# Two fused transformer blocks on one core: where the modulation products run

## The chip, the core and the metric

The kernel runs on one core of one Trainium2 chip, as one program of 31743 instructions. The metric is the device time of one execution in microseconds (us). Engines are called by the names of the profile: PE (TensorE, matmul), PEld (its weight loads), DVE (VectorE), ACT (ScalarE), POOL (GpSimd) and SP (SyncE, which here only issues transfers).

## The reference, cut to what matters

Two transformer blocks follow each other on 512 tokens of width 1024, in float32. The first block begins with a modulation: six vectors of 1024 numbers, made from a conditioning vector `c` and a 1024 x 6144 matrix.

```python
mod = jax.nn.silu(c) @ ada_w[l] + ada_b[l]
sh_m, sc_m, g_m, sh_f, sc_f, g_f = jnp.split(mod[:, None, :], 6, axis=-1)
h = rmsnorm(x, norm_g[l, 0]) * (1.0 + sc_m) + sh_m
p = h @ w_in[l]
...
x = x + g_m * rmsnorm(y, norm_g[l, 1])
h = rmsnorm(x, norm_g[l, 2]) * (1.0 + sc_f) + sh_f
f = conv_ffn(h, ffn_up[l], ffn_conv_w[l], ffn_conv_b[l], ffn_down[l])
x = x + g_f * rmsnorm(f, norm_g[l, 3])
```

`sh_m` and `sc_m` are wanted before the first projection; the other four are wanted only after the mixers. The mixers are a chunked RWKV recurrence (4 heads), a forgetting attention ("fox", 6 heads) and a sparse attention ("nsa", 6 heads, with compressed keys and values). The second block (a feed-forward, a token mixer, a feed-forward) uses no modulation, and nothing in it changes.

## The kernel before

**Layout.** Activations lie feature by token, in eight tiles of 128 features x 512 tokens. Each float32 operand of a projection is split into a high and a low part: `uh` and `ul` for activations, `whi` (ACT, L273) and `wlo` (DVE, L274) for weights. `dense` (L434) does three matmuls for each block of 128 x 128 weights. The weights come from one long stream of 128 x 1024 pieces, loaded by SP in program order into three buffers called `raw` (L268); `whi` and `wlo` have three buffers each.

**Front** (L543 to L601). Bias lines for the nsa bias come first (`lines`, L468): a one-hot table is loaded in four pieces of up to 512 columns, cast on POOL (L481), multiplied on PE, and written to DRAM (`d1`). The sum of squares of x gives the norm (`R`). Then for each of the eight feature blocks k, `products(k)` (L566) loads two 128 x 1024 pieces of the modulation matrix (`aw`, seven buffers) and multiplies them on PE, as 16 matmuls of 128 x 256 with a strip of 32 columns each (`silz`), into the bank `mps`. `modulate(k)` (L577) copies the strips (`am`), adds them up with four matmuls against a column of ones, and makes `mod`, `gf`, `uf` (DVE) and then `uh` (ACT) and `ul` (DVE). After that come 21 matmuls of block k into seven accumulators `kps` (called k in the profile). `products(k + 1)` is written ahead of the first of these, `modulate(k + 1)` ahead of the fourth.

**Preparation** (`prep`, L727, two head pairs), with projection matmuls as filler (`fill`, L949).

**Core** (loop over `core(t)`, L800, the chunk recurrence of the two head pairs). At each turn the loop takes a step of the recurrence, some filler projections (tile psm), and three steps of a side list: `decays`, `compress` (L990: tiles kk, kr, psa, ch, kct), then `fox` (L1102: tiles pss, p, pt). Every second turn `some_ada` (L616) emits one of the 16 late modulation units through `ada` (L503): two pieces of 128 x 1024 go into the same three `raw` buffers that the weight stream uses; the four terms of the first piece are made on DVE (one multiply, three multiply-adds), the first term of the second piece on ACT, and its other three on POOL (a multiply and an add each, L518 and L519), then one add joins both (L520). Two matmuls against ones (tile psr) and two adds give `mod`. In `compress`, POOL adds a position term to the gathered keys (`kr`, L1002). In `fox`, POOL scales the softmax rows (`p`, L1120). `load_cb` (L961) issues eight small transfers on POOL's queue.

What sets the order: the program is scheduled ahead of time by a list scheduler with priorities. Each engine then runs its own list strictly in order, so an instruction that waits holds all behind it on that engine; the same holds for transfers on SP's and POOL's queues.

Of the kernel before, what the change touches and what calls it, by code (L numbers as in the profile page):

```python
# [279 lines left out]
def two_blocks(ctx, tc, ins, out):  # L280
    nc = tc.nc
    S, V, G, PE = nc.scalar, nc.vector, nc.gpsimd, nc.tensor
    def mm(o, l, r, start=True, stop=True):
        PE.matmul(o, l, r, start=start, stop=stop)  # L284

    def act(o, i, f, **kw):
        S.activation(o, i, f, **kw)  # L287
# [10 lines left out]
    def stt(o, a, s, b, op0, op1):  # L298
        V.scalar_tensor_tensor(o, a, s, b, op0=op0, op1=op1)  # L299
# [156 lines left out]
    def lines_in(name, pool, rb, n, h, tiles=None):  # L456

        l = pool.tile([33, h], F32, name="rb" + name)
        V.memset(l[32:33, :], 1.0)
        (G if tiles else nc.sync).dma_start(l[:32, :], ins[rb])  # L460
        cols = []
        for j in range(0, n if tiles else 0, 512):
            m = min(512, n - j)
            cols.append(tiles()[:33, :m])
            G.dma_start(cols[-1], ins["lines" + name][:, j:j + m])
        return l, cols

    def lines(name, pool, o_tile, pst, n, h, dst, l, cols):  # L468

        hi, lo = [pool.tile([33, h], F32R, name="rb" + name + c) for c in "hl"]  # L470
        act(hi, l, AF.Copy)
        tt(lo, l, hi.bitcast(F32), SUB)
        for j in range(0, n, 512):
            m = min(512, n - j)
            if cols:
                o = cols.pop(0)
# [26 lines left out]
    def ada(dst, sec, k, raw, ap, bufs):  # L503

        am = [ap.tile([P, 256], F32, name=f"am{q}", bufs=bufs) for q in range(2)]
        for q in range(2):
            aw = raw()
            nc.sync.dma_start(aw.rearrange("p a b -> p (a b)"), ins["ada"][sec, k][:, q * 1024:(q + 1) * 1024])
            for r in range(4):
                s = sil[:, 4 * q + r:4 * q + r + 1]  # L510
                if q == 0 and r:
                    stt(am[0], aw[:, r], s, am[0], MUL, ADD)
                elif q == 0:
                    ts(am[0], aw[:, 0], s, None, MUL)
                elif r == 0:
                    act(am[1], aw[:, 0], AF.Copy, scale=s)
                else:
                    G.tensor_scalar(aw[:, r], aw[:, r], s, 1.0, op0=MUL, op1=MUL)  # L518
                    G.tensor_tensor(am[1], am[1], aw[:, r], op=ADD)  # L519
        G.tensor_tensor(am[1], am[0], am[1], op=ADD)  # L520
        for s in range(2):
            c = slice(s * P, (s + 1) * P)
            mm(dst[s], am[1][:, c], ones[:, 0:1])
# [16 lines left out]
    vcn = keep.tile([31, 2, 64], F32, name="vcn")  # L540
    cmask = keep.tile([P, 256], BF16, name="cmask")
    us = []
    AWB = 7  # L543
    with tc.tile_pool(name="lin", bufs=1) as lin, tc.tile_pool(name="p0", bufs=1, space=PSUM) as p0:
        x0 = part
        l1 = lines_in("1", keep, "rel_bias", E1_N, 6, lambda: lin.tile([P, T], F32, name="l1", bufs=4))
        for i in range(4):
            nc.sync.dma_start(x0[:, 2 * i:2 * i + 2], ins["x"][:, 2 * i:2 * i + 2])
        q0 = SqSum()
        for k in range(8):  # L550
            q0.add(x0[:, k])
        ps = row_sums(p0.tile([P, T], F32, name="nst", tag="x0"), [q0.acc])
        msx = const.tile([P, NB], F32, name="msx")
        V.tensor_copy(msx, ps[:, :NB])
        R = rms_bcast(p0, "x0", rsq(msx))
        kps = [p0.tile([P, T], F32, name=f"k{m}") for m in range(7)]
        spare = iter(kps[3:])
        lines("1", keep, lambda dt: lin.tile([P, T], dt, name="lo", bufs=3), lambda: next(spare), E1_N, 6, d1, *l1)
# [5 lines left out]
        mps, ws = [None] * 8, [None] * 8  # L564

        def products(k):  # L566


            mps[k] = p0.tile([P, T], F32, name="mps", tag="x0")
            for q in range(2):  # L570
                aw = lin.tile([P, 4, 256], F32, name="aw", bufs=AWB)
                nc.sync.dma_start(aw.rearrange("p a b -> p (a b)"), ins["ada"][0, k][:, q * 1024:(q + 1) * 1024])
                for r in range(4):
                    mm(mps[k][32 * r:32 * r + 32, :256], silz[:, 4 * q + r], aw[:, r], q == 0, q == 1)
            ws[k] = W.next("rwkv")

        def modulate(k):  # L577
            ps = mps[k]
            cp = lin.tile([P, 256], F32, name="am", bufs=2)
            V.tensor_copy(cp, ps[:, :256])  # L580
            for s in range(2):
                mm(ps[:, 256 + s:257 + s], cp[:, s * P:(s + 1) * P], ones[:, 0:1])
            tt(mod[:, k:16:8], ps[:, 256:258], vc("ada_b", 0, 16)[:, k::8], ADD)
            stt(gm[:, k:k + 1], mod[:, 8 + k:9 + k], 1.0, vc("norm_g", k), ADD, MUL)
            t = tmp("uf")
            stt(t, x0[:, k], gm[:, k:k + 1], R, MUL, MUL)
            us.append(cut_by(t, None, mod[:, k:k + 1], two(k)))

        products(0)
        modulate(0)  # L590
        for k in range(8):
            hi, lo = ws[k]
            for m in range(7):
                if k < 7 and m == 0:
                    products(k + 1)
                if k < 7 and m == 3:
                    modulate(k + 1)
                dense(kps[m], hi, lo, m * P, us[k:k + 1], k == 0, k == 7)
        for m in range(7):
            act(pr[m], kps[m], AF.Identity, scale=omu[:, m:m + 1])  # L600
            stt(pr[m][:, 1:], kps[m][:, :T - 1], vc("mu", m), pr[m][:, 1:], MUL, ADD)  # L601
# [11 lines left out]

    todo = [(sec, k) for sec in (1, 2) for k in range(8)]

    def some_ada(n=1):  # L616
        for _ in range(min(n, len(todo))):
            ps = bank(f"r{len(todo) % 2}", 2)
            sec, k = todo.pop(0)
            ada([ps[:, 0:1], ps[:, 1:2]], sec, k, lambda: wpool.tile([P, 4, 256], F32, name="raw", bufs=W.raw_bufs), st, 2)  # L620
            for s in range(2):
                j = (2 * sec + s) * 8 + k
                tt(mod[:, j:j + 1], ps[:, s:s + 1], vc("ada_b", j), ADD)

    def proj_t(label, evac):
        hi, lo = W.next(label)
# [333 lines left out]

    def load_cb():  # L961
        for p1 in range(8):
            G.dma_start(cb[p1 * 16:(p1 + 1) * 16],
                              bass.AP(tensor=d1[:].tensor, offset=d1[:].offset + LN + 7 - p1,
                                      ap=[[LC, 16], [E1_N, 6], [1, 55]]))

# [23 lines left out]
    def compress(spare):  # L990

        for j, nm in enumerate(("k", "v")):
            pe = vc("pe_" + nm, 0, 16)
            krs = [spare("kr") for _ in range(2)]
            for g in range(2):
                kk = spare("kk2")
                nc.sync.dma_start(kk[0:64], kcv[j][H2[g]])
                nc.sync.dma_start(kk[64:128, :T - 1], kcv[j][H2[g], 1:])
                kv = kk.rearrange("p (c j l) -> p c j l", j=8, l=2)[:, :, :, 0].rearrange("p c j -> p j c")
                for a in range(2):  # L1000
                    kr = krs[a][:, :496].rearrange("p (j g c) -> p j g c", g=2, c=31)
                    G.tensor_tensor(kr[:, :, g], kv[:, :, a:a + 31],  # L1002
                                    pe[:, 8 * a:8 * a + 8, None].to_broadcast([P, 8, 31]), op=ADD)
            ps = bank("a", 1)
            for q in range(4):
                w1 = spare("w1")
# [95 lines left out]
    def fox(j, spare):  # L1102
# [7 lines left out]
        for i in range(NB):  # L1110
# [3 lines left out]
            for s in range(2):  # L1114
                ps = pS()
                mm(ps[:, :n], fq[j][H2[s], qs], fk[j][H2[s], :n], True, False)
                mm(ps[:, qs], cmask[:, :P], cmask[:, P:], False, True)
                p = tmp("p")
                r = soften([(ps[:, :n], fb[s][:, :n])], p)
                G.tensor_scalar(p[:, :n], p[:, :n], r, 1.0, op0=MUL, op1=MUL)  # L1120
                yield
                pts.append(flip(p, n, spare("pt")))
            yield
# [309 lines left out]
    def raw(name, k, s, hl):  # L1433

        return cut_by(x[k][:, s], vc(name, k), None, hl, s)
# [597 lines left out]
```

## Time and profile before

| | |
|---|---|
| time, median of 3 runs | 2218.21 us (2211.95, 2218.21, 2218.94) |
| the profiled execution's own time | 2212.43 us |
| its span, first to last instruction | 2210.6 us |
| PE busy | 2140.8 us (97%) |
| DVE busy | 1141.6 us (52%) |
| ACT busy | 787.0 us (36%) |
| POOL busy | 440.7 us (20%) |

A busy share is a mean over the whole span. The stages differ, so the profile is read by stretch: the front ends at 80.68 us, when the first matmul into psm begins; the core begins at about 133 us and ends at about 376 us; from 600 us to the end PE is busy almost without a gap. "Idle before" with a name behind an arrow is the time that an engine stood still, and what it was waiting for. PEclk is the granted clock of TensorE, 1.00 for 2.4 GHz and 0.50 for 1.2 GHz.

### The profile page before, as it was taken

The numbers are of one execution on the slowest core, as the hardware profiler recorded it, in microseconds if no ns is written. First come the engines' busy times: TensorE is split into PE (matmuls) and PEld (weight loads), VectorE is DVE, ScalarE is ACT, GpSimd is POOL, SyncE is SP. The second block draws the span as 40 slices with busy tenths as digits, with TensorE's granted clock in tenths as the row PEclk, the third lists the DMA queues.
The fourth block names the chain that finished last, engine by engine and source line by source line (L and its number), as shares of the span: only waits on it lengthen the run. The fifth ranks groups of instructions, "written<-read, shape, count | busy, mean of one in ns | idle before, by whom it ended". The sixth has DMA issues, their size and how long they took to land.

```text
span 2210.6 us, 31743 instructions
## 1 busy us (share of the span) xinstructions
PE 2140.8 (97%) x12572; PEld 1761.8 (80%) x12572; DVE 1141.6 (52%) x2191; ACT 787.0 (36%) x1326; POOL 440.7 (20%) x444
## 2 busy tenths in 40 slices
PE   7988999998999999899999999999999999999999
PEld 4777776766788888888888889998877888888887
DVE  4563544657653465654344439967645455433442
ACT  3332233553543343332222335445443233222221
POOL 2043343235000000221011023343221022100110
PEclk9987998998999999999999999999999999999999
DMA  8244233301452222132222343243162223322222
GB/s 318 77 141 148 97 135 97 113 1 32 151 181 97 96 95 96 58 109 101 96 95 95 119 142 113 92 139 96 67 186 68 101 85 101 103 96 96 96 95 86
DMA packets 84319, 238.32 MB, mean 108 GB/s; under 512 B 13270, under 2 KB 20887, under 8 KB 84042
## 3 DMA queue, kind: packets, MB, share of 16 engines
q1 hardware_dynamic: 77978, 226.03, 31.0%
q0 software_dynamic: 5472, 9.69, 1.3%
q8 instruction: 99, 1.62, 0.3%
q10 hardware_dynamic: 720, 0.57, 0.1%
q14 instruction: 50, 0.41, 0.1%
HBM read 216.02 MB, written 15.33 MB: 105 GB/s over the span
## 4 chain that ended last, share of the span: by engine, by line
PE 89%; DVE 4%; DMA 2%; POOL 1%; ACT 1%; issue 1%; SPq 1%; ACTq 0%; DVEq 0%; POOLq 0%
PE mm L284 66%; PE psm L284 4%; PE psr L284 3%; PE pS L284 3%; PE pss L284 2%; PE k L284 2%; PE pO L284 2%; PE pso L284 2%; PE pT L1618 1%; PE pst L1079 1%; PE psa L284 1%; DMA raw<-in_ada_dram 1%; PE pT L1601 1%; DVE ul L299 0%; PE mps L284 0%
## 5 line engine op out<-in xcount | busy, mean ns | idle before, releaser
L273 ACT ACTIVATE whi<-raw 128x1024 fp32r<-128x1024 f32 (+4 forms) x314 | 327.9, 1046 | 813.5 <-PE mm L284 616.1
L274 DVE TENSOR_TENSOR wlo<-raw,whi 128x1024 fp32r<-128x1024 f32 (+4 forms) x302 | 371.0, 1230 | 328.4 <-ACT whi L273 322.1
L284 PE MATMUL mm<-ul,whi 128*128 128x512 f32 (+1 forms) x1296 | 501.8, 388 | 6.3 <-DVE ul L299 6.3
L284 PE MATMUL mm<-uh,wlo 128*128 128x512 f32 (+1 forms) x1296 | 500.9, 387 | 1.0 <-DVE wlo L274 1.0
L284 PE MATMUL mm<-uh,whi 128*128 128x512 f32 (+1 forms) x1296 | 496.2, 388 | 4.7 <-ACT uh L287 3.7
L284 PEld LDWEIGHTS mm<-ul,whi 128*128 128x128 f32 x1296 | 244.9, 189 | 59.3 <-DVE ul L299 9.4
L284 PEld LDWEIGHTS mm<-uh,whi 128*128 128x128 f32 x1296 | 242.8, 189 | 56.2 <-ACT uh L287 5.3
L284 PEld LDWEIGHTS mm<-uh,wlo 128*128 128x128 f32 x1296 | 244.9, 189 | 50.9 <-DVE wlo L274 1.9
L284 PE MATMUL mm<-hl,whi 128*128 128x512 f32 (+1 forms) x550 | 209.3, 381 | 0.0
L284 PE MATMUL mm<-hh,wlo 128*128 128x512 f32 (+1 forms) x550 | 209.3, 381 | 0.0
L284 PE MATMUL mm<-hh,whi 128*128 128x512 f32 (+1 forms) x550 | 208.4, 381 | 0.0
L1469 POOL TENSOR_TENSOR gg<-gg,R 128x512 f32<-128x512 f32 x44 | 77.1, 1756 | 473.7 <-ACT gg L287 473.7
L284 PE MATMUL mm<-whi,uh 128*128 128x256 f32 (+1 forms) x488 | 140.5, 288 | 0.0
L284 PE MATMUL mm<-whi,ul 128*128 128x256 f32 (+1 forms) x488 | 139.8, 287 | 0.0
L284 PE MATMUL mm<-wlo,uh 128*128 128x256 f32 (+1 forms) x488 | 139.2, 285 | 0.0
L284 PEld LDWEIGHTS mm<-hl,whi 128*128 128x128 f32 x550 | 103.4, 188 | 19.8
L284 PEld LDWEIGHTS mm<-hh,whi 128*128 128x128 f32 x550 | 103.4, 188 | 19.7
L284 PEld LDWEIGHTS mm<-hh,wlo 128*128 128x128 f32 x550 | 103.4, 188 | 19.7
L287 ACT ACTIVATE p<-p,smin 128x128 f32<-128x128 f32 (+4 forms) x136 | 81.8, 602 | 83.8 <-DVE smin L1055 48.3
L290 DVE TENSOR_TENSOR gh<-mm,gg 128x512 f32<-128x512 f32 x44 | 30.4, 691 | 130.7 <-PE mm L284 125.2
L284 PEld LDWEIGHTS mm<-whi,ul 128*128 128x128 f32 x488 | 93.2, 191 | 1.7 <-issue 1.5
L284 PEld LDWEIGHTS mm<-whi,uh 128*128 128x128 f32 x488 | 93.0, 191 | 1.4 <-issue 0.4
(512 smaller groups left out, 3354.6 us busy)
## 6 DMA issues: line engine op xcount, KB each, us to landing
raw<-in_wst_dram SPq DMA_DIRECT2D x294, 512.0 KB
raw<-in_ada_dram SPq DMA_DIRECT2D x32, 512.0 KB
aw<-in_ada_dram SPq DMA_DIRECT2D x16, 512.0 KB
raw<-in_wst_dram SPq DMA_DIRECT2D x8, 448.0 KB
ka<-d POOLq DMA_DIRECT2D x1, 3570.0 KB, 51.2
k<-d POOLq DMA_DIRECT2D x1, 2556.0 KB, 20.7
part<-in_x_dram SPq DMA_DIRECT2D x4, 512.0 KB
xa<-in_x_dram SPq DMA_DIRECT2D x8, 256.0 KB
```

The costliest lines, as they stand in the source:

```text
L273: nc.scalar.activation(hi[:, :n], w, AF.Copy)
L274: (e or nc.vector).tensor_tensor(lo[:, :n], w, hi[:, :n].bitcast(F32), op=ALU.subtract)
L284: PE.matmul(o, l, r, start=start, stop=stop)
L287: S.activation(o, i, f, **kw)
L290: V.tensor_tensor(o, a, b, op=op)
L1079: PE.transpose(ps[:, j:j + P], p[:, j:j + P], ident)
L1469: G.tensor_tensor(g, g, R, op=MUL)
L1601: PE.transpose(ps[:, (j * nb + b) * P:(j * nb + b + 1) * P], xn[:, (b * n + j) * P:(b * n + j + 1) * P], ident)
L1618: PE.transpose(ps[:, j:j + P], p[:, o + j:o + j + P], ident)
```

## The change

1. Front, modulation. Blocks 0 to 2 keep the strips on PE. For blocks 3 to 7 the products move: four terms to DVE, four scalings to ACT, and the adding up to POOL. `products` now runs two blocks ahead, and the strips of blocks 0 and 1 use banks of accumulators that are not needed yet (`kps[6]`, `kps[5]`).
2. Front, bias lines. The one-hot table comes in one transfer; the short last piece is multiplied first; only two banks are used for it. (The order of the pieces changes for the second block's table too.)
3. Core, late modulation. All eight terms of a unit are made on POOL, in 15 instructions; the matmuls against ones are written one unit later than before (`owing`).
4. Core, `kr` and the scaling of `p` in `fox` move from POOL to DVE; `load_cb` moves from POOL's queue to SP's.

```diff
@@ lines_in, lines
-        for j in range(0, n if tiles else 0, 512):
...
+            t = tiles()
+            G.dma_start(t, ins["lines" + name])
...
-        for j in range(0, n, 512):
+        js = [*range(0, n, 512)]
+        for j in js[-1:] + js[:-1]:
@@ front
-    AWB = 7
+    AWB, STRIPS = 7, 3
...
-        spare = iter(kps[3:])
+        spare = iter(2 * kps[3:5])
...
-            mps[k] = p0.tile([P, T], F32, name="mps", tag="x0")
+            mps[k] = kps[6 - k] if k < 2 else p0.tile([P, T], F32, name="mps", tag="x0")
+            am = ams[k] = lin.tile([P, 256], F32, name="am", bufs=2)
...
-                    mm(mps[k][32 * r:32 * r + 32, :256], silz[:, 4 * q + r], aw[:, r], q == 0, q == 1)
+                    s = sil[:, 4 * q + r:4 * q + r + 1]
+                    if k < STRIPS:
+                        mm(mps[k][32 * r:32 * r + 32, :256], silz[:, 4 * q + r], aw[:, r], q == 0, q == 1)
+                    elif q == 0:
+                        if r:
+                            stt(am, aw[:, r], s, am, MUL, ADD)
+                        else:
+                            ts(am, aw[:, 0], s, None, MUL)
+                    elif r == 0:
+                        am1 = lin.tile([P, 256], F32, name="am1", bufs=2)
+                        act(am1, aw[:, 0], AF.Copy, scale=s)
+                    else:
+                        act(aw[:, r], aw[:, r], AF.Copy, scale=s)
+                        G.tensor_tensor(am1, am1, aw[:, r], op=ADD)
+            if k < STRIPS:
+                V.tensor_copy(am, mps[k][:, :256])
+            else:
+                G.tensor_tensor(am, am, am1, op=ADD)
...
-        products(0)
-        modulate(0)
+        for k in range(2):
+            products(k)
+        for k in range(2):
+            modulate(k)
...
-                if k < 7 and m == 0:
-                    products(k + 1)
-                if k < 7 and m == 3:
+                if k < 6 and m == 0:
+                    products(k + 2)
+                if 0 < k < 7 and m == 3:
                     modulate(k + 1)
@@ some_ada (ada is gone)
+            if todo:
+                sec, k = todo.pop(0)
+                am = st.tile([P, 256], F32, name="am", bufs=4)
...
+                        if q + r == 0:
+                            G.tensor_scalar(am, aw[:, r], s, 1.0, op0=MUL, op1=MUL)
+                            continue
+                        G.tensor_scalar(aw[:, r], aw[:, r], s, 1.0, op0=MUL, op1=MUL)
+                        G.tensor_tensor(am, am, aw[:, r], op=ADD)
+                owing.append((sec, k, am))
+            if len(owing) > 1 or not todo:
+                sec, k, am = owing.pop(0)
+                ps = bank(f"r{k % 2}", 2)
...
@@ load_cb, compress, fox
-            G.dma_start(cb[p1 * 16:(p1 + 1) * 16],
+            nc.sync.dma_start(cb[p1 * 16:(p1 + 1) * 16],
...
-                    G.tensor_tensor(kr[:, :, g], kv[:, :, a:a + 31],
-                                    pe[:, 8 * a:8 * a + 8, None].to_broadcast([P, 8, 31]), op=ADD)
+                    tt(kr[:, :, g], kv[:, :, a:a + 31],
+                                    pe[:, 8 * a:8 * a + 8, None].to_broadcast([P, 8, 31]), ADD)
...
-                G.tensor_scalar(p[:, :n], p[:, :n], r, 1.0, op0=MUL, op1=MUL)
+                ts(p[:, :n], p[:, :n], r, None, MUL)
```

How the order moves. First PE's list at the start of the front, from the norm's broadcast (nbc) to the first matmul of block 0 (mps and k_189 hold strips, ones against am adds them up). Before:

```order
L376 MATMUL nbc<-cm,rb 128x128 x4
L284 MATMUL mps<-aw,silz 32x256 x8
L284 MATMUL mps<-ones,am 128x1 x2
L284 MATMUL mps<-aw,silz 32x256 x8
L284 MATMUL k_189<-uh,whi 128x512
```

and now, from the first strip:

```order
L284 MATMUL k_189<-aw,silz 32x256 x4
L284 MATMUL nst<-ones,acc 128x1 x4
L284 MATMUL k_186<-lo,rb1h 6x512
L284 MATMUL k_186<-lo,rb1l 6x512
L284 MATMUL k_189<-aw,silz 32x256 x4
L284 MATMUL k_188<-aw,silz 32x256 x4
L376 MATMUL nbc<-cm,rb 128x128 x4
L284 MATMUL k_189<-ones,am 128x1 x2
L284 MATMUL k_188<-aw,silz 32x256 x4
L284 MATMUL mps<-aw,silz 32x256 x4
L284 MATMUL k_188<-ones,am 128x1 x2
```

Three half strips (12 of the 20 instructions) now stand ahead of nbc; behind it come two more halves, two additions of strips, two bias matmuls (k_187) and then block 0.

Second, POOL's list where the late modulation begins in the core. Before, three multiplies, three adds and a joining add for a unit:

```order
L518 TENSOR_SCALAR raw<-raw,sil 128x256 x3
L519 TENSOR_TENSOR am_1286<-am_1286,raw 128x256 x3
L520 TENSOR_TENSOR am_1286<-am_1285,am_1286 128x256
L518 TENSOR_SCALAR raw<-raw,sil 128x256 x3
L519 TENSOR_TENSOR am_1382<-am_1382,raw 128x256 x3
```

and now:

```order
L631 TENSOR_SCALAR am<-raw,sil 128x256
L633 TENSOR_SCALAR raw<-raw,sil 128x256 x3
L634 TENSOR_TENSOR am<-am,raw 128x256
L633 TENSOR_SCALAR raw<-raw,sil 128x256 x2
L634 TENSOR_TENSOR am<-am,raw 128x256
L633 TENSOR_SCALAR raw<-raw,sil 128x256 x2
L634 TENSOR_TENSOR am<-am,raw 128x256 x5
```

A unit is now 15 instructions on POOL, and adds of the first piece stand behind multiplies of the second.

Third, DVE's list in the core where the compressed keys are finished (ch, cu and kct). Before:

```order
L290 TENSOR_TENSOR ch<-cu,ch 128x62
L294 TENSOR_SCALAR am_2245<-raw,sil 128x256
L299 SCALAR_TENSOR_TENSOR am_2245<-raw,sil,am_2245 128x256 x3
L1028 COPY kct<-psa 128x31
L290 TENSOR_TENSOR mod<-psr_1696,vec 128x1 x2
```

and now:

```order
L290 TENSOR_TENSOR ch<-cu,ch 128x62
L1046 COPY kct<-psa 128x31
L274 TENSOR_TENSOR wlo<-raw,whi 128x1024
L290 TENSOR_TENSOR mod<-psr_1727,vec 128x2
```

The four modulation instructions that stood between ch and kct are gone from DVE's list.

## Rows read from the trace of the kernel before

**Rows 1.** Busy us (and instructions) of each engine by stretch, granted clock, DMA:
```profile
25.45:80.68 55.23, 50.56 (x299) 37.84 (x295) 25.30 (x52) 14.58 (x20) 5.00 (x10) 1.00 0.54 188
...
150.00:210.00 60.00, 48.06 (x579) 41.75 (x580) 27.62 (x58) 13.27 (x21) 31.37 (x43) 0.74 0.57 178
210.00:240.00 30.00, 28.23 (x469) 23.89 (x467) 13.35 (x38) 6.73 (x16) 10.17 (x19) 0.89 0.31 105
...
360.00:380.00 20.00, 18.48 (x79) 11.51 (x78) 10.75 (x27) 4.72 (x11) 6.76 (x6) 0.54 0.18 47
...
600.00:2210.00 1610.00, 1597.28 (x8207) 1349.48 (x8205) 811.48 (x1372) 564.36 (x850) 257.12 (x194) 1.00 0.32 104
```

**Rows 2.** Timeline of PE, front: start us, us, operation, count, idle before:
```profile
18.07 1.08 PE L376 MATMUL nbc<-cm,rb 128*128 128x128 f32 x4 [1.14 <-issue]
19.84 1.93 PE L284 MATMUL mps<-aw,silz 128*32 128x256 f32 x16 [0.69 <-ACT R L287]
...
25.45 2.44 PE L284 MATMUL k<-uh,whi 128*128 128x512 f32 x6
...
39.13 1.07 PE L284 MATMUL mps<-aw,silz 128*32 128x256 f32 x16
...
72.91 0.50 PE L284 MATMUL mps<-ones,am 128*128 128x1 f32 x4
75.78 1.89 PE L284 MATMUL k<-uh,whi 128*128 128x512 f32 x7 [2.37 <-ACT uh L287]
```

**Rows 3.** Timeline of ACT, front: the weights of blocks 0 and 2 arrive:
```profile
14.89 0.95 ACT L273 ACTIVATE whi<-raw 128x896 fp32r<-128x896 f32 x1 [2.01 <-DMA raw<-in_wst_dram]
...
22.14 0.95 ACT L273 ACTIVATE whi<-raw 128x896 fp32r<-128x896 f32 x1 [1.51 <-DMA raw<-in_wst_dram]
```

**Rows 4.** Groups of DVE by shape, 24 to 80 us: busy us, mean ns:
```profile
L274 DVE TENSOR_TENSOR wlo<-raw,whi 128x896 fp32r<-128x896 f32 x6 | 6.5, 1088 | 3.3 <-ACT whi L273 3.3
L299 DVE SCALAR_TENSOR_TENSOR ul<-uf,mod,uh 128x512 fp32r<-128x512 f32 x8 | 6.0, 746 | 2.4 <-ACT uh L287 2.4
L299 DVE SCALAR_TENSOR_TENSOR uf<-part,gf,R 128x512 f32<-128x512 f32 x8 | 5.9, 736 | 0.3
```

**Rows 5.** Groups of DVE by shape, core (133 to 378 us):
```profile
L299 DVE SCALAR_TENSOR_TENSOR am<-raw,sil,am 128x256 f32<-128x256 f32 x48 | 24.8, 516 | 1.1
...
L294 DVE TENSOR_SCALAR am<-raw,sil 128x256 f32<-128x256 f32 x16 | 7.0, 435 | 33.8 <-DMA raw<-in_ada_dram 23.5 <-POOL am L520 10.3
...
L290 DVE TENSOR_TENSOR AK<-psr,x 128x512 f32<-128x512 f32 x4 | 2.6, 678 | 0.0
```

**Rows 6.** Groups of POOL by shape, core (133 to 378 us):
```profile
L519 POOL TENSOR_TENSOR am<-am,raw 128x256 f32<-128x256 f32 x48 | 39.0, 813 | 23.7 <-ACT am L287 21.4
L518 POOL TENSOR_SCALAR raw<-raw,sil 128x256 f32<-128x256 f32 x48 | 24.8, 534 | 59.8 <-DMA raw<-in_ada_dram 23.2 <-DVE am L299 22.7 <-DVE cu L296 9.2
L520 POOL TENSOR_TENSOR am<-am,am 128x256 f32<-128x256 f32 x16 | 11.7, 733 | 0.9
```

**Rows 7.** Waits of PE, 133 to 380 us: total us, times, longest:
```profile
PE psa L284 <- DVE kct L1028: 6.1, 1, 6.1
PE pss L1079 <- POOL p L1120: 3.1, 3, 1.5
PE psr L284 <- DVE part L290: 2.4, 1, 2.4
...
PE psa L284 <- POOL kr L1002: 1.7, 1, 1.7
```

**Rows 8.** Timeline of DVE, core, around kct:
```profile
193.36 0.35 DVE L294 TENSOR_SCALAR am<-raw,sil 128x256 f32<-128x256 f32 x1 [7.21 <-POOL am L520]
```

**Rows 9.** Timeline of POOL, core: first and last joining add (of 16), last power:
```profile
143.65 0.74 POOL L520 TENSOR_TENSOR am<-am,am 128x256 f32<-128x256 f32 x1
...
343.21 0.74 POOL L520 TENSOR_TENSOR am<-am,am 128x256 f32<-128x256 f32 x1
...
361.31 1.65 POOL L710 TENSOR_TENSOR hr<-hv,mhalf 128x8 f32<-128x8 f32 x1 [3.58 <-DVE hv L294]
```

More of the change, by code (lines that the diff above doesn't have):

```diff
@@ L461, in lines_in @@
         cols = []
-        for j in range(0, n if tiles else 0, 512):
-            m = min(512, n - j)
-            cols.append(tiles()[:33, :m])
-            G.dma_start(cols[-1], ins["lines" + name][:, j:j + m])
+        if tiles:
+            t = tiles()
+            G.dma_start(t, ins["lines" + name])
+            cols = [t[:, j:min(j + 512, n)] for j in range(0, n, 512)]
         return l, cols
@@ L472, in lines @@
         tt(lo, l, hi.bitcast(F32), SUB)
-        for j in range(0, n, 512):
+        js = [*range(0, n, 512)]
+        for j in js[-1:] + js[:-1]:
             m = min(512, n - j)
             if cols:
-                o = cols.pop(0)
+                o = cols[j // 512]
             else:
@@ L501, in skewed @@
                        ap=[[n - 1, P]] + ([[P * n, nh]] if nh else []) + ap)
[L503 to L523, printed above, removed]
     ks, kw = [keep.tile([P, T], F32, name=n) for n in ("ks", "kw")]
@@ L542, in two_blocks @@
     us = []
-    AWB = 7
+    AWB, STRIPS = 7, 3
     with tc.tile_pool(name="lin", bufs=1) as lin, tc.tile_pool(name="p0", bufs=1, space=PSUM) as p0:
         x0 = part
-        l1 = lines_in("1", keep, "rel_bias", E1_N, 6, lambda: lin.tile([P, T], F32, name="l1", bufs=4))
+        l1 = lines_in("1", keep, "rel_bias", E1_N, 6, lambda: lin.tile([33, E1_N], F32, name="l1"))
         for i in range(4):
@@ L564, in two_blocks @@
         mps, ws = [None] * 8, [None] * 8
+        ams = [None] * 8
         def products(k):
-            mps[k] = p0.tile([P, T], F32, name="mps", tag="x0")
+            mps[k] = kps[6 - k] if k < 2 else p0.tile([P, T], F32, name="mps", tag="x0")
+            am = ams[k] = lin.tile([P, 256], F32, name="am", bufs=2)
             for q in range(2):
@@ L573, in products @@
                 for r in range(4):
-                    mm(mps[k][32 * r:32 * r + 32, :256], silz[:, 4 * q + r], aw[:, r], q == 0, q == 1)
+                    s = sil[:, 4 * q + r:4 * q + r + 1]
[16 more added lines that the diff above has]
+                G.tensor_tensor(am, am, am1, op=ADD)
             ws[k] = W.next("rwkv")
         def modulate(k):
-            ps = mps[k]
-            cp = lin.tile([P, 256], F32, name="am", bufs=2)
-            V.tensor_copy(cp, ps[:, :256])
+            ps, cp = mps[k], ams[k]
             for s in range(2):
@@ L614, in two_blocks @@
     todo = [(sec, k) for sec in (1, 2) for k in range(8)]
+    owing = []
     def some_ada(n=1):
[L617 to L623, printed above, removed]
+        for _ in range(n):
+            if not todo and not owing:
+                return
+            if todo:
+                sec, k = todo.pop(0)
+                am = st.tile([P, 256], F32, name="am", bufs=4)
+                for q in range(2):
+                    aw = wpool.tile([P, 4, 256], F32, name="raw", bufs=W.raw_bufs)
+                    nc.sync.dma_start(aw.rearrange("p a b -> p (a b)"), ins["ada"][sec, k][:, q * 1024:(q + 1) * 1024])
+                    for r in range(4):
+                        s = sil[:, 4 * q + r:4 * q + r + 1]
+                        if q + r == 0:
[7 more added lines that the diff above has]
+                ps = bank(f"r{k % 2}", 2)
+                for s in range(2):
+                    mm(ps[:, s:s + 1], am[:, s * P:(s + 1) * P], ones[:, 0:1])
+                j = 16 * sec + k
+                tt(mod[:, j:j + 9:8], ps[:, :2], vc("ada_b", j, 9)[:, ::8], ADD)
     def proj_t(label, evac):
@@ L1001, in compress @@
                     kr = krs[a][:, :496].rearrange("p (j g c) -> p j g c", g=2, c=31)
-                    G.tensor_tensor(kr[:, :, g], kv[:, :, a:a + 31],
-                                    pe[:, 8 * a:8 * a + 8, None].to_broadcast([P, 8, 31]), op=ADD)
+                    tt(kr[:, :, g], kv[:, :, a:a + 31], pe[:, 8 * a:8 * a + 8, None].to_broadcast([P, 8, 31]), ADD)
             ps = bank("a", 1)
```

## Prediction

> **What bounds the kernel now.** I read the busy shares by stretch first [rows 1]. From 600 us to the end TensorE stands still for 12.7 us in 1610: nothing there can gain, and the change doesn't touch it. Three stretches have room. In the front, from block 0's first matmul (25.45) to the projections (80.68), TensorE is busy for 50.56 of 55.23 us, all of it at full clock; only work taken away from it, or the 4.67 us of idle time, can shorten this. In the core, from 150 to 210 us, it is busy for 48.06 of 60 us, and at a mean granted clock of 0.74: between the levels 0.50 and 1.00 that is about half of the time, some 31 us, at 1.2 GHz. Work done at 1.2 GHz takes twice as long, so with 48.06/60 of the 31 us busy (25 us), up to 12 us are lost to the clock, beside 11.9 us of idle time. From 210 to 240 the clock is 0.89 and the idle time 1.8 us. The tail of the core (360 to 380 us, clock 0.54) loses time too, but the change doesn't reach it.
>
> The next view is the timeline of the front [rows 2]. The reader is to see four things: the strips of a block cost 1.07 us at full clock (39.13), its adding up 0.50 us (72.91); block 0 starts 7.4 us after the norm's broadcast (18.07), with strips and additions between; and at 75.78 TensorE waits 2.37 us for `uh` of the last block. Then the list of TensorE's waits in the core [rows 7]: one of 6.1 us for `kct`, which only DVE holds up. The timeline of DVE [rows 8] says why: the first modulation multiply, at 193.36, had waited 7.21 us for a joining add on POOL, and `kct`'s copy stands behind it. Waits for `p` (3.1) and `kr` (1.7) come from POOL too.
>
> **The front, part by part.** My sum starts from the profiled execution (2212.43 us); the median is 5.8 above it.
>
> Dense matmuls of the eight blocks: 50.56 us of work, less six strips (6 x 1.07 = 6.4) and seven additions (7 x 0.50 = 3.5), leave 40.6 us, 5.1 for a block [rows 1, 2]. They stay. Strips of blocks 3 to 7 go: 5 x 1.07 = 5.35 us. Block 2's second half (0.5 us) and six additions (3.0 us) remain in the stretch.
>
> Start of block 0. Three of the five half strips fit ahead of the broadcast, two of them into idle time and the third at about 0.97 us (half of the 1.93 of 19.84), so that the broadcast ends some 0.8 later, at about 19.9. Behind it come 0.5 + 0.97 + 0.97 + 0.5 for two halves and two additions, and some 0.9 for two bias matmuls: first matmul at about 24.0, 1.5 earlier. Bounds: no gain if the chain to `uh` (DVE and ACT) ends last, and 2.5 if the strips hide wholly. The bias lines in one load and in other banks are otherwise hidden: their matmuls need to be done only when the core reads `d1`.
>
> The stall for `uh` of 2.37 us stays, one block sooner: TensorE's list puts the additions of blocks 6 and 7 together, just ahead of block 6. I carry 2.4, with bounds of 0 and 5.
>
> So the front ends at 24.0 + 40.6 + 0.5 + 3.0 + 2.4 = 70.5 instead of 80.68: **10 us gained**, 6 to 13.5 by the bounds.
>
> What hides the work moved: DVE makes for each of blocks 3 to 7 one multiply (0.435) and three multiply-adds (3 x 0.516), 1.98 us by the same instructions in the core [rows 5], on top of `wlo`, `ul` and `uf` (1.09 + 0.75 + 0.74, [rows 4]); with 0.3 for two tiny ones 4.9 us, under 5.1 + 0.5 of TensorE. It fits, with 0.7 to spare. ACT gets four scalings of the same shape as DVE's 0.435 us (I take half a us each), POOL three adds and one join, 3 x 0.81 + 0.73 = 3.2 us a block [rows 6]; both were idle most of the stretch [rows 1]. Transfers keep up: `raw` of block 0 arrives at 14.9, of block 2 at 22.1 [rows 3], 3.6 us a block against 5.6 of TensorE.
>
> **The core, part by part.** Removed from DVE: 16 units of 0.435 + 3 x 0.516, 31.7 us [rows 5]. Added: eight `kr` of at most 0.68 each (the nearest two-input row is 128 x 512) and 24 `p` of 0.44 to 0.68: 16 to 22 us. Its net load falls by some 10 to 16 us, but the gain is in the order: nothing on DVE waits for POOL's modulation now, and between `ch` and `kct` nothing stands. ACT loses 16 scalings.
>
> POOL. One unit was 3 x 0.534 + 3 x 0.813 + 0.733 = 4.8 us; it becomes 8 x 0.534 + 7 x 0.813 = 10.0 us [rows 6], 159 us for 16, less what `kr` and `p` took. The joins run from 143.65 to 343.21, 13.3 us a unit [rows 9], so POOL is busy for three quarters of that pace. What waits for POOL: the `raw` buffers, which the weight stream shares; the additions (one unit later in the list, which makes slack); and at the end the power for `hr`, which stands behind all units on POOL's list. It starts at 361.31 and the last join ends at 343.95, so the units may end 17.4 us later before it moves.
>
> The Trainium skill speaks against this move: "GPSIMD Engine Reference", section Engine selection, sends elementwise work on a tile to VectorE, with GpSimd about 2 times slower for two-input operations. The trace agrees and goes further, since 0.534 + 0.813 on POOL does what one DVE instruction does in 0.516, 2.6 times; by that rule alone the core would get slower.
>
> The stalls: `kct` 6.1 + `p` 3.1 + `kr` 1.7 = 10.9 us are touched directly. `kct`'s wait ends at once when its copy follows `ch`; the others become waits for DVE, which has less in its list. What is late next is the weight stream, because POOL frees the `raw` buffers more slowly, and the `psr` additions (2.4 us). A stretch with fewer stalls may also keep the clock up, as the stretch after 600 us does (1.00, hardly a gap): 12 us are at stake between 150 and 210 [rows 1]. Together some 23 us are touched; I take **10 gained**, close to the directly named waits, with bounds of 20 (both the waits and most of the clock) and of -8 (the buffers held by POOL stop the weight stream for half a us in each unit). `load_cb` on SP's queue: eight small issues behind `raw` loads that are far ahead, hidden; if they weren't, the queue's delay would be some 3 us once.
>
> Sum: 2212.4 - 10 - 10 = 2192.4. From the median the same gain gives 2198. I put the forecast at **2196**, between the two.
>
> **The rivals.**
> 1. *Front alone.* The waits of the core are replaced by others of the same size (a `psr` or `raw` wait where `kct` stood) and the clock stays at 0.74. For it: the list of the core is rebuilt by the scheduler, and stalls there are spread over many sources. Against: the longest one has a named cause that is taken away. Result: 2218.2 - 10 or 2212.4 - 10, say 2205, from 2200 to 2211.
> 2. *DVE binds the front.* The four modulation instructions stand in order among `uf`, `ul` and `wlo`, so an `aw` that lands late holds `ul` of another block, and each of five blocks waits a us or two for it. For it: only 0.7 us to spare a block. Against: transfers are ahead [rows 3]. The front then gains 2 to 4 instead of 10, and with an unchanged core the time is 2213, from 2210 to 2217, within what a measurement of this kernel can tell from no change, about 0.3%.
> 3. *The POOL train* (the slower side). All eight terms stand on one engine, in order, and wait for their transfers; a transfer waits for a `raw` buffer that POOL itself frees. If this loop costs 6 us for each unit on top of the 10.0 of work, units come every 16 us: 15 x 2.7 = 40 us later at the end, 17.4 of them free, so `hr` and all behind it move by 23 us, and with the front's gain the time is 2218 - 10 + 23 = 2231. It decides from about 5 us of idle time per unit. For it: POOL waited 23.2 us for `raw` transfers before its multiplies already [rows 6], and DVE 23.5 [rows 5]. Against: that is 1.5 us a unit, not 6; and half of the 59.8 us was waiting for DVE, which falls away.
> 4. *It doesn't do what it says.* A blocked instruction takes the place of the modulation multiply on DVE: `p`'s scaling or `kr`, waiting for gathered keys, stands ahead of `kct` or a state copy, and POOL's unloading gains nothing. Then the core loses a wait of the size of 6.1 for another, and the result is rival 1's.
>
> **How the numbers follow.** Forecast 0.58, from 2182 to 2204. Rival 1 with 4: 0.20, 2200 to 2211. Rival 2: 0.12. Rival 3: 0.10, 2225 to 2240. The range reaches from 2180 (front 13, core 20) to 2212, which takes in rival 1 and the lower part of rival 2, and leaves out about 0.18. Faster by over 0.3% means under 2211.6: 0.58 + 0.20 less a little, and some of rival 2, 0.79. Within: 0.12. Slower, over 2224.9: 0.09.
>
> **What would show it.** In the front: first matmul into k at about 24; strips only up to block 2; psm's first matmul near 70.5; one wait for `uh` ahead of block 6 and none ahead of block 7. If waits of 1 us for `uh` stand in each of blocks 3 to 7, rival 2 holds. In the core: no `kct` wait on DVE; the last `am` add on POOL at 335 or earlier; `hr` waiting for `hv` as now and not starting behind a unit; granted clock above 0.74 in the 60 us after the start of the compressed keys. If the units come more than 15 us apart and projections wait for `wlo` or `whi`, with SP's queue waiting for POOL, rival 3 holds. The forecast is wrong if the front ends after 74, or if the distance from the front's end to the power for `hr` is not at least 5 us shorter than the 280.6 us of before.

## The result, and the profile after

The changed kernel takes 2192.15 us (median of four runs, 2190.00 to 2193.31), the kernel before 2215.08 us in the same comparison (2211.39 to 2218.94): a ratio of 0.990, 95% interval 0.988 to 0.992, so 23 us faster. The prediction was 2196, range 2180 to 2212. In the profiled executions the span fell from 2210.6 to 2190.0 us, by 20.6; the profiled execution of before (2212.43 us) was one of its faster ones.

To see where the time went, the span is cut at five events that both traces have: block 0's first matmul (k<-uh,whi), the first matmul into psm, the last step of the preparation (psr<-rk,x), the power for `hr` at the end of the recurrence (the first of its last two), and the first psm matmul after it.

| stretch, us | before | after | change | forecast |
|---|---|---|---|---|
| start to block 0's first matmul | 25.45 | 24.28 | -1.2 | -1.5 |
| front, block 0 to psm | 55.23 | 48.66 | -6.6 | -8.7 |
| preparation | 44.81 | 44.76 | 0 | 0 |
| core, recurrence (to `hr`) | 235.82 | 230.99 | -4.8 | -10 for both |
| core, tail (`hr` to its end) | 18.87 | 14.06 | -4.8 | |
| the rest | 1830.42 | 1827.25 | -3.2 | 0 |

The rows of the changed kernel are, in order: the front, the 60 us that answer to 150 to 210 of before (both about 25 us into the core), the recurrence and the tail. Columns are those of [rows 1], after the name of the stretch: length, then busy us (and instructions) of PE, PEld, DVE, ACT and POOL, granted clock, DMA share, GB/s.

```profile
24.28:72.94 48.66, 45.56 (x201) 36.38 (x201) 36.85 (x63) 23.44 (x41) 21.61 (x23) 0.96 0.62 224
...
142.00:202.00 60.00, 50.56 (x672) 44.10 (x670) 21.00 (x36) 10.26 (x16) 51.37 (x82) 0.77 0.55 171
...
117.70:348.69 230.99, 219.10 (x2621) 172.86 (x2621) 103.68 (x230) 66.43 (x130) 151.61 (x240) 0.93 0.41 136
348.69:362.75 14.06, 14.06 (x62) 8.90 (x60) 7.68 (x18) 3.86 (x8) 5.78 (x4) 0.61 0.46 113
```

The reader is to see POOL in the second row: busy for 51.4 of 60 us, where it was 31.4 before. The mean over the whole core hides this. TensorE gained 2.5 us of busy time there, and its clock is 0.77, not much above 0.74.

The front, from the timeline of TensorE (start, length, operation, count, idle before and what ended it), against [rows 2]:

```profile
24.28 2.50 PE L284 MATMUL k<-uh,whi 128*128 128x512 f32 x5
...
45.32 0.50 PE L284 MATMUL k<-ul,whi 128*128 128x512 f32 x1 [1.16 <-DVE ul L299]
...
60.15 0.61 PE L284 MATMUL mps<-ones,am 128*128 128x1 f32 x4 [0.98 <-DVE gf L299]
61.71 3.36 PE L284 MATMUL k<-uh,whi 128*128 128x512 f32 x7 [0.95 <-ACT uh L287]
```

No strips stand behind block 2. Three waits are left, 3.1 us in all: one in block 3, one between the two additions ahead of block 6, and one between them and block 6 itself. Behind these the seven matmuls of block 6 take 3.36 us where those of [rows 2] took 1.89: the mean granted clock in the 4.65 us from there is 0.64, between its levels 0.50 and 1.00.

The waits of TensorE in the core (total us, times, longest), against [rows 7]:

```profile
PE psa L284 <- DVE ch L290: 5.8, 1, 5.8
PE psa L284 <- DMA w<-in_ck_dram: 2.8, 2, 2.4
PE psr L284 <- DVE rk L299: 1.9, 1, 1.9
PE psm L284 <- ACT nq L287: 1.5, 1, 1.5
...
PE pss L1097 <- DVE p L294: 0.4, 1, 0.4
```

The wait for `kct` is gone, those for `p` have shrunk to 0.4 us; a wait for `ch` of nearly the same size has come. The timeline of DVE says why, against [rows 8]:

```profile
177.35 1.14 DVE L290 TENSOR_TENSOR kr<-kk,vec 128x248 f32<-128x248 f32 x2 [8.24 <-DMA kk<-kcv]
178.41 0.14 DVE L290 TENSOR_TENSOR mod<-psr,vec 128x2 f32<-128x2 f32 x1
178.48 0.21 DVE L1034 COPY ch<-psa 128x62 f32<-128x62 f32 x1
```

`kr`, which the change moved to DVE, waits 8.24 us for gathered keys, and `ch` of the group before stands behind it.

POOL at the end of the units, against [rows 9]:

```profile
318.54 7.14 POOL L634 TENSOR_TENSOR am<-am,raw 128x256 f32<-128x256 f32 x8
348.69 1.65 POOL L729 TENSOR_TENSOR hr<-hv,mhalf 128x8 f32<-128x8 f32 x1 [23.02 <-DVE hv L294]
```

The last unit ends at 325.7, 23 us ahead of `hr`. From the end of the first (139.1) that is 12.4 us a unit, against 13.3 before.

### The profile page after: what moved, and what is told of

It is laid out like the page before. It is cut to its first block, busy times and chain, and to the rows that moved or that the text cites. A ratio compares the mean times of both kernels' runs of the same rounds, so it can differ in the third digit from the quotient of the medians.

```text
span 2190.0 us, 31626 instructions
## 1 busy us (share of the span) xinstructions
PE 2132.7 (97%) x12492; PEld 1758.9 (80%) x12492; DVE 1145.0 (52%) x2158; ACT 787.1 (36%) x1330; POOL 513.5 (23%) x549
## 4 chain that ended last, share of the span: by engine, by line
PE 87%; POOL 4%; DMA 4%; DVE 3%; issue 1%; ACT 1%; SPq 0%; POOLq 0%; DVEq 0%; ACTq 0%
PE mm L284 67%; PE psm L284 4%; PE pS L284 3%; PE psr L284 2%; DMA raw<-in_ada_dram 2%; POOL am L634 2%; PE pO L284 2%; PE pss L284 2%; PE k L284 2%; PE pso L284 1%; POOL raw L633 1%; PE pT L1636 1%; PE pst L1097 1%; DMA raw<-in_wst_dram 1%; DVE ul L299 1%
## 5 line engine op out<-in xcount | busy, mean ns | idle before, releaser
L284 PEld LDWEIGHTS mm<-ul,whi 128*128 128x128 f32 x1296 | 245.1, 189 | 58.7 <-DVE ul L299 8.7
```

## The experiments

Each kernel's median stands beside the kernel before on the same chip (2216.62, 2215.00 and 2216.53 us in the three groups of four); ratios have 95% intervals. The differences to the changed kernel are between medians of different groups, and each interval reaches 2 to 7 us to either side, so differences of three or four us mean nothing. The scheduler makes new lists for every kernel, and stretches differ by some us with them; so stretches are read rather than sums. All stretches in this table are from the traces, one of each kernel, cut as above.

| kernel | median us | ratio to before | front | recurrence | tail | rest |
|---|---|---|---|---|---|---|
| before | 2215.1 | 1 | 55.23 | 235.82 | 18.87 | 1830.42 |
| changed | 2192.2 | 0.988 to 0.992 | 48.66 | 230.99 | 14.06 | 1827.25 |
| e1 front only | 2206.9 | 0.9945 to 0.9974 | 54.90 | 232.02 | 17.40 | 1834.97 |
| e2 core only | 2205.8 | 0.9936 to 0.9968 | 57.48 | 231.37 | 13.12 | 1829.95 |
| e3 `kr` on POOL | 2196.8 | 0.9892 to 0.9935 | 49.24 | 236.75 | 14.92 | 1827.90 |
| e4 `p` on POOL | 2214.3 | 0.9982 to 1.0003 | 48.98 | 236.41 | 27.31 | 1830.43 |
| e5 front and `load_cb` | 2197.9 | 0.9893 to 0.9932 | 48.95 | 235.78 | 10.54 | 1830.25 |
| e6 `load_cb` on POOL | 2199.5 | 0.9903 to 0.9938 | 55.41 | 230.72 | 12.80 | 1826.83 |
| e7 modulation shared | 2194.7 | 0.9876 to 0.9919 | 49.14 | 225.67 | 15.31 | 1832.54 |
| e8 `p` alone | 2212.5 | 0.9977 to 1.0000 | 57.42 | 237.03 | 10.43 | 1839.04 |
| e9 before, fox ahead | 2215.5 | 0.9988 to 1.0011 | 57.38 | 250.37 | 9.83 | 1827.26 |
| e10 changed, fox ahead | 2207.1 | 0.9946 to 0.9975 | 48.88 | 244.46 | 10.61 | 1831.59 |
| e11 more POOL work | 2225.2 | 1.0011 to 1.0073 | 49.03 | 259.49 | 12.28 | 1832.62 |
| e12 shared, fox ahead | 2199.8 | 0.9909 to 0.9949 | 48.73 | 241.69 | 8.95 | 1829.79 |

### The two parts alone (e1, e2)

e1 takes the edits of the front from the change and leaves the rest as before; e2 takes the edits of the core (`some_ada`, `kr`, `p`, `load_cb`).

> The kernel before with the change's front alone (strips of blocks 0 to 2 on TensorE, bias lines in one load); the core as before. Theory A (the two parts add up): front ends at about 73 us instead of 80.68, the core keeps its length of 254.7 us (from the matmul psr<-rk,x at 125.49 to the first psm of the tail at 380.18), so 7 to 8 us faster than before, about 2207. Rival B (the front's gain is lost in the core, since the core's transfers and POOL work start no earlier): front ends at 73, the core is longer by as much, within 3 us of before.

> The kernel before with the change's core alone (late modulation on POOL, kr and p on DVE, load_cb on SP's queue); the front as before. Theory A: front ends at 80.7, the core is about 10 us shorter and the rest 3 us shorter, so 12 to 15 us faster than before, about 2201. Rival B (the core's gain needs the earlier start of the front): 0 to 6 us faster. Rival C (the longer POOL units bind once they start no earlier): units more than 13 us apart, no gain.

e1: 9.7 us faster by the medians, but the front, which I expected to end at 73, ended at 80.25. POOL's timeline in the front of e1 shows what ate most of the gain:

```profile
41.74 3.61 POOL L984 DMA_DIRECT2D cb<-d  x7
53.27 0.52 POOL L984 DMA_DIRECT2D cb<-d  x1 [7.92 <-DMA k<-d]
53.80 1.53 POOL L591 TENSOR_TENSOR am<-am,aw 128x256 f32<-128x256 f32 x2
55.42 0.72 POOL L595 TENSOR_TENSOR am<-am,am 128x256 f32<-128x256 f32 x1
```

and TensorE waits for these adds:

```profile
56.19 0.79 PE L284 MATMUL mps<-ones,am 128*128 128x1 f32 x4 [2.54 <-POOL am L595]
59.36 1.01 PE L284 MATMUL mps<-ones,am 128*128 128x1 f32 x4 [2.38 <-POOL am L595]
```

The eighth transfer of `load_cb` stands still for 7.92 us until the skewed bias rows (k<-d) are written. In the kernel before POOL had no adds in the front; now those of blocks 5 to 7 stand behind it. So the front of the change brings little without the edit that I had put under the core. e2 is 10.8 us faster, theory A in the core (10.2 us shorter, about 10 expected) and not in the sum (12 to 15; the rest is 0.5 us shorter and not 3): its recurrence and tail are those of the changed kernel. It does not follow that the waits went: e2 still waits 7.2 us for `kct` and 4.9 for `kr`.

### `load_cb` (e5, e6)

```diff
-            G.dma_start(cb[p1 * 16:(p1 + 1) * 16],
+            nc.sync.dma_start(cb[p1 * 16:(p1 + 1) * 16],
```

e5 is e1 with this line; e6 is the changed kernel without it.

> The kernel before with the change's front and load_cb on SP's queue; the rest of the core as before. With the front alone POOL's queue stood 7.9 us at load_cb, which waited for the skewed bias rows (k<-d), with the adds of blocks 5 to 7 behind it; TensorE waited 2.5 and 2.4 us for them, and the front ended at 80.25. Theory A (load_cb on POOL's queue is what ate the front's gain): no wait for an add of POOL, front ends at 72 to 74, 4 to 7 us faster than the front alone, 2200 to 2203. Rival B (the adds are late for another reason, DVE or ACT): front ends at 77 or later, within 3 us of the front alone.

> The changed kernel with load_cb back on POOL's queue. Theory A: the adds of blocks 5 to 7 stand behind load_cb again, two waits of about 2.5 us for am, front ends at 78 to 80 instead of 72.94, 4 to 7 us slower than the changed kernel, 2196 to 2199. Rival B (load_cb's place on the queue doesn't matter in the whole change): within 2 us of the changed kernel.

Both went as theory A has it. Adding the line takes the front from 54.90 to 48.95 us, taking it out makes 48.66 into 55.41; the medians move by 9.0 and 7.3 us, or by 7.4 both times if each is taken from the kernel before in its own group. In e6 the cause stands in the list of waits of the front:

```profile
PE mps L284 <- POOL am L573: 5.4, 2, 3.0
```

On SP's queue the issues wait too, and the next load of weights stands behind them until 52.63; but none of TensorE's waits in the front is for weights. SP's timeline in the front of the changed kernel:

```profile
36.99 13.38 SPq L982 DMA_DIRECT2D cb<-d  x7
52.63 0.35 SPq L269 DMA_DIRECT2D raw<-in_wst_dram  x1
53.02 0.43 SPq L982 DMA_DIRECT2D cb<-d  x1
```

### `kr` and `p` back on POOL (e3, e4)

> The changed kernel with kr back on POOL. In the trace of the changed kernel DVE stood 8.24 us ahead of a kr that waited for gathered keys, with ch behind it, and TensorE waited 5.8 us for ch. Theory A (kr on DVE put a new wait in the place of the one for kct): the 5.8 us wait goes, 3 to 6 us faster than the changed kernel, about 2187. Rival B (the keys are late whoever adds to them): TensorE waits as long for kr itself, and POOL's units stand behind it: within 2 us of the changed kernel or up to 4 slower.

> The changed kernel with the scaling of p in fox back on POOL, where it now stands among units of 10 us. Theory A: the waits for p (3.1 us in the kernel before) come back and grow, since a p can stand behind a run of up to eight adds: 3 to 10 us slower than the changed kernel, 2195 to 2202. Rival B (the list places p well, and DVE had room either way): within 2 us of the changed kernel.

e3 is 4.6 us slower than the changed kernel by the medians, near rival B, but the intervals overlap (0.9892 to 0.9935 and 0.988 to 0.992); the gain of theory A did not come. The wait for `ch` is gone as I thought, but waits of 4.0 us for `kr` on POOL, 4.1 for weights of the compressor (w) and 4.4 for `fk` on ACT took its place. The keys are late whoever adds to them; the wait moves with the instruction.

e4 is 22 us slower than the changed kernel, with everything else in place: the way of theory A, but far beyond its 3 to 10 us; only e11 costs more. TensorE waits for `p` in the core, and the tail is twice as long:

```profile
PE pss L1097 <- POOL p L1138: 11.6, 4, 6.9
```

```profile
355.36:382.67 27.31, 23.02 (x85) 13.04 (x84) 10.95 (x29) 6.37 (x14) 7.33 (x7) 0.54 0.19 49
```

DVE's timeline shows why the tail grew: the two softmaxes of the last fox step (128x512) come 13.3 and 20.2 us after the power for `hr` (355.36), where the last came 1.5 us after it in the changed kernel and 10.2 us after it in the kernel before.

```profile
368.66 0.69 DVE L1073 CUSTOM_DVE_ANT_0 p<-pss,fb 128x512 f32<-128x512 f32 x1 [1.66 <-PE pss L284]
...
375.60 0.69 DVE L1073 CUSTOM_DVE_ANT_0 p<-pss,fb 128x512 f32<-128x512 f32 x1 [2.90 <-PE pss L284]
```

In this tail TensorE is busy for 23.0 of 27.3 us, at a mean clock of 0.54. The tail is 13 of the 22 us; the recurrence has 5.4 more.

### The modulation itself, and `p` without it (e7, e8)

e7 is the changed kernel with `ada` and `some_ada` of before; e8 is the kernel before with one line, `ts(p[:, :n], p[:, :n], r, None, MUL)` in the place of POOL's scaling.

> The changed kernel with the late modulation shared among DVE, ACT and POOL as before (front, kr, p and load_cb changed). Theory A (the modulation on POOL alone is what frees DVE, and carries the core's gain): multiplies that wait for POOL stand in DVE's list again, a wait of 4 us or more for kct or ch, 8 to 14 us slower than the changed kernel, 2200 to 2206. Rival B (p and kr off POOL carry it): within 4 us of the changed kernel.

> The kernel before with the scaling of p in fox on DVE and nothing else changed. In the changed kernel p back on POOL cost 22 us. Theory A (p's place among units of 10 us was the cost, so without these units it matters little): 0 to 4 us faster than the kernel before, its 3.1 us of waits. Rival B (p on POOL is costly in any list): 8 us or more faster.

e7 takes 2194.69 us, within rival B's 4 us of the changed kernel, and the intervals overlap (0.9876 to 0.9919 and 0.988 to 0.992): the edit that the change is named for, all late modulation on POOL, can't be told from nothing here. The multiplies that wait stand in DVE's list again, but the wait of TensorE for `kct` is 0.5 us and that for `ch` 1.0. e8 gains 2.5 us by the medians, 5 at most by the interval (0.9977 to 1.0000), theory A: moving `p` is worth little by itself, and 22 us where POOL has units of 10 us.

### Fox steps ahead of the recurrence's end (e9, e10, e12)

The tail seemed to follow from where the last fox step falls. So:

```diff
-        for _ in range(NS):
+        for _ in range(NS + (turn[0] > 17)):
```

in the kernel before (e9), in the changed one (e10) and in e7 (e12).

> The kernel before with one change: from turn 18 of the core on, four steps of the side list in a turn instead of three, so that the last fox softmax (128x512) stands ahead of the power for hr on DVE's list (it ran 10.2 us behind it). Nothing of the case's change is in it. Theory A (the core's end is set by fox steps left over when the recurrence is done; where these fall decides much of the core's time in all runs so far): from hr to the core's end 10 to 12 us instead of 18.87, 5 to 8 us faster than before, 2207 to 2210, with the kct wait of 6 us still there. Rival B (the steps only move, and TensorE waits for them earlier): core within 2 us of 254.7, same time as before.

> The changed kernel with the same edit (four side steps from turn 18 on). Its last fox softmax ran 1.5 us behind hr, so there is less to gain. Theory A: from hr to the core's end 10 to 12 us instead of 14.06, 2 to 4 us faster than the changed kernel, about 2189. Rival B: within 1 us of it or slower.

> The changed kernel with the late modulation shared among DVE, ACT and POOL as before, and four side steps from turn 18 on. Its core was the shortest of all (240.98 us), with 15.3 us from hr to the end. Theory A (both gains add up): from hr to the end 10 to 12 us, core about 237, 3 to 5 us faster than the shared kernel, 2190 to 2192, at or below the changed kernel. Rival B (moving fox ahead costs as much in the recurrence): within 2 us of the shared kernel, 2194.

All three tails shrank, about as theory A has it (to 9.8, 10.6 and 9.0 us), and all three recurrences grew by more: 14.6, 13.5 and 16.0 us. e9 in the two stretches, recurrence and tail:

```profile
127.04:377.41 250.37, 232.23 (x2652) 180.40 (x2652) 119.80 (x283) 77.57 (x153) 98.22 (x146) 0.90 0.40 130
377.41:387.24 9.83, 8.63 (x31) 4.83 (x30) 6.58 (x16) 0.63 (x1) 3.26 (x2) 0.60 0.51 135
```

Rival B holds in kind: the steps only move. Its sizes did not all hold: the core of e9 is 260.2 us and not within 2 of 254.7, though its time came out even by the median, and e10 and e12 cost 15 and 5 us. A fox step moved ahead of the end is paid for in the recurrence, so a short tail is no gain by itself, and where the changed kernel's comes from is not settled by these runs.

### How close POOL is to binding (e11)

```diff
                        G.tensor_scalar(aw[:, r], aw[:, r], s, 1.0, op0=MUL, op1=MUL)
+                        G.tensor_scalar(aw[:, r], aw[:, r], 1.0, 1.0, op0=MUL, op1=MUL)
```

> The changed kernel with seven more multiplies by 1.0 in each late unit on POOL (3.7 us a unit by 0.534 us each, some 60 us in all; the products stay the same). Theory A (POOL has room: its last unit ended 24 us ahead of hr): units 12 to 14 us apart at the most, the last add ends at 335 to 355, 0 to 6 us slower than the changed kernel. Rival B (the train of units is already close to what binds: transfers wait for buffers that POOL holds): core 20 us longer or more, 2212 or above.

33 us slower than the changed kernel: rival B. The last add ends at 350.2, inside the stretch that theory A gave, and 28.3 us ahead of `hr` (378.50), so the end of the units is not what binds. The trace shows another path, in the stretch from 180 to 200 us:

```profile
180.00:200.00 20.00, 7.95 (x105) 6.90 (x105) 1.33 (x2) 2.63 (x4) 18.34 (x34) 0.75 0.45 146
```

POOL is busy for 18.3 of 20 us, TensorE for 8.0. Twice ACT waits for weights that SP could not load, and TensorE stands behind it, the first time for 12.05 us, the second for 9.9 us by way of DVE's `wlo`:

```profile
195.59 1.06 ACT L273 ACTIVATE whi<-raw 128x1024 fp32r<-128x1024 f32 x1 [12.83 <-DMA raw<-in_wst_dram]
...
219.03 1.06 ACT L273 ACTIVATE whi<-raw 128x1024 fp32r<-128x1024 f32 x1 [14.97 <-DMA raw<-in_wst_dram]
```

```profile
197.67 0.79 PE L284 MATMUL psm<-uh,whi 128*128 128x512 f32 x1 [12.05 <-ACT fq L287]
```

SP's loads of weights (L269) waited for POOL's adds, which hold the `raw` buffers that both use: 30.2 us in the changed kernel, 51.7 us here, by the waits of SP's queue:

```profile
SPq L627 <- POOL am L635: 76.7, 22, 12.1
SPq L269 <- POOL am L635: 51.7, 10, 13.3
```

No kernel of the study beats the changed one.

## Why the prediction was right, point by point

**The front: right, one edit priced wrongly.** TensorE's work was 45.56 us against 44.1 worked out; the 1.5 us over are block 6's first matmuls (3.36 us against 1.89) at a clock of 0.64. Idle time was 3.1 against 2.4. The end, 72.94, lies 2.4 us after the forecast and inside its bounds.

Other traces qualify this. Seven more kernels of the study have this front with `load_cb` on SP's queue: their fronts end at 72.5 to 74.3, five of them after 74, from where on I had called the forecast wrong. Block 0 began at 24.28 (forecast 24.0), but with the new front it begins at 23.7 to 25.4 and with the old one at 24.7 to 25.5, so no gain at the start is shown, and 24.28 is luck. And the front of before, 55.23 us, is the shortest of its kind: e2, e8 and e9 have the same front code, e2 but for the queue of `load_cb`, and take 57.4 or 57.5. Against these the eight new fronts (48.7 to 49.2 us) gain 8.2 to 8.8 us, as forecast (8.7).

What I had wrong is `load_cb`: "hidden; if they weren't, the queue's delay would be some 3 us once". That priced the move from the side where it went and not from the side that it left. Left on POOL's queue it costs the front 6.0 to 6.8 us (e1 against e5, e6 against the changed kernel), most of the gain. Rival 2, DVE binding the front, did not come: two waits name DVE, of 1.16 and 0.98 us, and the second is as much POOL's, whose joining add ends 0.06 us ahead of the matmul that waited.

**The core: right in size (9.6 us against 10), wrong in how it came.** My step was that the waits for `kct`, `p` and `kr` (10.9 us) go. Rival 4's blocked instruction did come in their place, 5.8 us behind a `kr` that waits for keys. And e5 keeps the old core with a wait of 6.6 us for `kct`, and its core (recurrence and tail) is 246.3 us, 8.4 shorter than before and within 1.3 of the changed kernel's 245.1. The cores of before, of the changed kernel and of e5, with the same number of matmuls but for one:

```profile
125.49:380.18 254.69, 237.79 (x2680) 184.46 (x2680) 123.96 (x301) 77.81 (x154) 100.81 (x148) 0.88 0.39 127
117.70:362.75 245.05, 233.16 (x2681) 181.76 (x2681) 111.37 (x248) 70.29 (x138) 157.39 (x244) 0.91 0.42 135
118.83:365.15 246.32, 229.12 (x2681) 178.66 (x2681) 124.44 (x300) 76.96 (x153) 101.97 (x148) 0.93 0.41 132
```

The changed kernel's core has 5.0 us less idle time than before (11.9 against 16.9) and 4.6 us less busy time, at a mean clock of 0.91 instead of 0.88. In e5 the idle time is no smaller (17.2), and the whole gain is busy time, 8.7 us less at a clock of 0.93. So the waits are about half of where the time is, and adding up the named ones to the whole gain was the step that failed; the size came out by luck, since the clock, which I had only in the upper bound, gave the other half. By place, half of the gain lies in the tail, of which I wrote that the change doesn't reach it.

**The modulation on POOL: harmless, not helpful.** Its list had room at the end (23 us of waiting ahead of `hr`), the units came 12.4 us apart, and the clock in the 60 us was 0.77: the signs that I gave against rival 3 all held. But e7 shows no gain by it that can be told from nothing, and e4 with e8 that it makes the move of `p` necessary. The Trainium skill ("GPSIMD Engine Reference", section Engine selection) sends elementwise work on a tile to VectorE; the runs agree in that POOL earns nothing with it (e7) and stands near its bound (e11), although that rule alone would have forecast a slower kernel.

**Rival 3's threshold was wrong.** I had it decide from about 5 us of idle time a unit, by the average pace over the core and the slack ahead of `hr`. e11 puts 3.7 us of work on a unit and loses 33. The binding place is earlier, where POOL is busy for 51 of 60 us in the changed kernel and holds buffers that the weights need; the average of three quarters over the core hid it. The forecast's 0.09 for slower was too small for how near it was.

**The test that I gave myself.** The distance from the front's end to `hr` was to be at least 5 us shorter than 280.6; it is 275.75, 4.9 shorter, so by its letter the test failed, if by 0.1 us. The sum held since the tail gave 4.8 us and the rest 3.2, neither forecast: the total is better than its parts, and that is luck.

**Open.** The same core code gives cores of 246.3 (e5), 249.4 (e1) and 254.7 us (before), with TensorE busy for 229.1, 235.2 and 237.8 us at clocks of 0.93, 0.91 and 0.88. So the busy time makes most of the difference, but why the clock differs was not found, nor why the rest of the kernel varies from 1826.8 to 1839.0 us. The lists of the scheduler differ in each, and e9, e10 and e12 show that moving fox ahead does not shorten the core. No kernel was traced twice, so what changes between two executions of one kernel can't be told from what its list does. By the medians the front with `load_cb` (e5) carries 17 of the 23 us; some 6 to 8 of these are explained, in the front, and the others are seen in the trace by place, not by cause. What the core's edits add to e5, 6 us by the medians, is not clear of the intervals. No run separates the edit of the bias lines from that of the strips.

## What to carry to other kernels

When an engine gets new urgent work, look at everything else in its list, above all at transfers that wait for other transfers: moving such an issue elsewhere can be worth more than the arithmetic that was moved. A wait named in the trace is not yet a gain: the instruction behind it may wait as long for the next thing, so look for what comes next in the new list before counting it, and compare TensorE's busy time and clock beside its waits. And to find how near an engine is to binding, read its busy share in its densest stretch and ask whose buffers it holds; a mean over the stage says little.

## What the runs showed of the hardware

The same instructions after the same wait ran at different clocks in different executions. In the front of the kernel before, the seven matmuls of block 7 took 1.89 us after a wait of 2.37 us [rows 2]; in e2, whose front has the same code but for the queue of `load_cb`, they took 3.25:

```profile
75.93 3.25 PE L284 MATMUL k<-uh,whi 128*128 128x512 f32 x7 [2.37 <-ACT uh L287]
```

The granted clock from there to the first psm matmul was 1.00 in the one:

```profile
75.78:80.68 4.90, 4.90 (x22) 4.05 (x22) 2.79 (x6) 2.52 (x5) 0.00 (x0) 1.00 0.18 62
```

and 0.74 in the other, a mean between its two levels, 1.00 and 0.50:

```profile
75.93:82.45 6.52, 6.52 (x21) 5.18 (x22) 2.84 (x6) 2.57 (x5) 0.00 (x0) 0.74 0.15 46
```

e8 and e9 have this front too, and there the seven took 3.35 us after the same wait of 2.37. So in four traces the fall of the clock came three times and stayed away once, and it is worth 1.6 us. The four are different kernels with the same front; that one kernel does either from execution to execution is likely and not shown. It may be one reason why the profiled execution of before lies below its median.
